# Values of two strided attention patterns by seven half-size products instead of eight, with sums of weights kept in DRAM

## Chip, core and metric

One core of a Trainium2 chip runs the whole program: a hybrid layer (block 1), then two layers of attention and retention (block 2), for 512 tokens of width 1024. The metric is device time in microseconds (us) of one execution; the lower, the better. TensorE is called PE, VectorE DVE, ScalarE ACT, GpSimd POOL, and SyncE SP: SP issues nearly all DMAs, in one queue and in its program order.

## What is computed

Only one projection of block 2 is touched. In each of its two layers the normalized input `h` (512 x 1024) is multiplied by `w_in`, and the columns called `va` (1536 of them) are the attention's values, 512 for each of three patterns:

```
ATT_PATTERNS = ((128, 1), (512, 4), (2048, 16))
...
h = rmsnorm(x, norm_w) * (1.0 + scale[:, None, :]) + shift[:, None, :]
proj = h @ w_in
qa, ka, va, za, qr, kr, vr, zr, ga, gr = jnp.split(proj, SPLIT_POINTS, axis=-1)
...
qa, ka, va = qa.reshape(att_shape), ka.reshape(att_shape), va.reshape(att_shape)
```

The first pattern is dense (g=0 in the kernel); the other two (g=1 and g=2) have strides of 4 and 16 and want their tokens regrouped by the token's number modulo 4. So the product in question is `h` (512 x 1024) times 1024 columns of weights, once in each layer.

## The kernel before

Every fp32 product is made of three products of rounded parts: `split` (lines 140 to 148) copies a tile to fp32r on ACT, the high part, and subtracts that copy from the tile on DVE, the low part; then high x high, high x low and low x high are summed in PSUM. A matmul with 512 columns is the unit of PE's work.

Weights come in tiles of 128 x 1024 fp32, 512 KB. `load_w` (line 187) takes one: a DMA into a raw tile `wr`, of which there are two, then `wh` on ACT (L144) and `wl` on DVE (L145), of which there are four pairs and, for each fifth load, one more. A raw tile is free for the next DMA when its `wl` is made. A pair is free when the last matmul that reads it has run. In nearly all stages one weight tile serves 24 matmuls.

`T_` (line 222) makes an output of 512 tokens by 512 columns in four PSUM banks, one for each 128 tokens, from four weight tiles. `attention_v` (line 961) calls it once for g=0, with all four weight tiles loaded first and each group of tokens started as its norm comes ready, and then, from inside `attention` (L1122), for g=1 and g=2 one weight tile after the other: 96 matmuls each, and for each group of 128 tokens a copy on ACT and four DMAs of 64 KB that regroup the tokens (L973, L975). Behind these come the q and k products of the heads (`w2_qk`).

In the first layer `rotary_tables` (line 925) makes sines and cosines for the retention, some 17 operations on DVE and two on ACT, just ahead of those products.

The feed-forward stage of block 1 (`ffn`, line 739) runs 44 weight tiles. Beside it a second task, `ada` (line 570), multiplies a vector by 25 MB of modulation weights on DVE: tiles `aw` of 256 KB through SP's queue, each followed by one DVE operation (L578). Tasks are generators that yield an estimated time; `tick` resumes them between matmuls. After that the framework orders the instructions of each engine by its own estimates, where `high_priority` pulls the weight loads ahead. What stands in an engine's queue behind an instruction that waits has to wait too.

Of the kernel before, what the change touches and what calls it, by code (L numbers as in the profile page):

```python
# [7 lines left out]
F32 = mybir.dt.float32  # L8
F32R = mybir.dt.float32r
I32 = mybir.dt.int32  # L10
AF = mybir.ActivationFunctionType
# [4 lines left out]
P = 128  # L16
S = 512
D = 1024
# [32 lines left out]
class Block:  # L51
# [211 lines left out]
    def T2_(self, lhs, srcs, nk, done, room, mid=None, cut=None):  # L263

        npair = nk // 2
        banks = [[None] * 4, [None] * 4]

        def step(half, t, w, c, kk, a=0, b=512):
            k = 2 * c + kk
            o = slice(kk * 512 + a, kk * 512 + b)
            if banks[half][t] is None:
                banks[half][t] = self.pst()
            ps = banks[half][t][:, a:b]
            hi, lo = lhs(k, t, 0), lhs(k, t, 1)
# [12 lines left out]
        if mid:  # L290
            mid()
        spare = iter(room())
        sets = [(half, c) for half in range(2) for c in range(first[half], npair)]
        ws = {x: self.load_w(srcs[x[0]][x[1]], next(spare, None)) for x in sets}
        for t in range(4):
            for half in range(2):
                parts = (0, 256, 512) if cut and t == 3 and half else (0, 512)
                for a, b in zip(parts, parts[1:]):
                    if a:
                        banks[half][t] = None  # L300
                    for c in range(first[half], npair):
                        for kk in range(2):
                            step(half, t, ws[half, c], c, kk, a, b)
                    if len(parts) > 2:
                        cut(banks[half][t], a, b)
                    else:
                        done(t, half, banks[half][t])

    def room(self, x):

# [428 lines left out]
    def ffn(self, hf, fp, es_w):  # L739
        tc, nc, A, v = self.tc, self.nc, self.A, self.nc.vector  # L740
        f, th = [], {}
        es = ExitStack()
        pool = []

        def done(i, ps):
# [77 lines left out]
    def block2(self, h, es_w):  # L823
# [6 lines left out]
        for l in range(2):  # L830
# [4 lines left out]
            yp, e_ya = op("yatt")  # L835
            ya = self.new_op(yp, "ya", n=4)
            vp, e_v = op("attv")
            V = self.attention_v(l, h, vp, range(1))
# [117 lines left out]
        nc.scalar.activation(self.cos, k, AF.Sin)  # L956


    def attention_v(self, l, h, vp, gs, V=None, ap=None):

        V = {} if V is None else V
        for g in gs:
            if g:
                for c in range(4):
                    V[g, c] = vp.tile([P, 512], F32, tag="V", name=self.nm("V"), bufs=12)

            def done(t, ps):
                if g == 0:
                    V[g, t] = vp.tile([P, 512], F32, tag="V", name=self.nm("V"), bufs=12)
                    self.nc.scalar.activation(V[g, t], ps, AF.Copy)  # L970
                    return
                x = ap.tile([P, 512], F32, tag="qk", name=self.nm("Vt"), bufs=4)
                self.nc.scalar.activation(x, ps, AF.Copy)  # L973
                for c in range(4):
                    self.nc.sync.dma_start(out=V[g, c][t * 32:t * 32 + 32, :], in_=x[c:P:4, :])  # L975

            self.T_(self.tok(h), self.A["w2_va"][l, g], 8, done, outer=0 if g else 4, ready=None if g else h.ready)
        return V

    def attention(self, l, h, ap, vp, V, ya, mrg):  # L980

# [133 lines left out]
        def finish(rows_):  # L1115
            while not all(r.done for r in rows_):
                yield 0.5
            yield from join()
            for hd in range(4):
                yield from out(hd)  # L1120

        self.attention_v(l, h, vp, (1, 2), V, ap)  # L1122
        for hd in range(4):
            head(hd, range(3))
        self.spawn(finish(list(self.tasks)))
        for i in range(12):
            if i % 3 == 0:
# [526 lines left out]
```

## Time and profile before

| | us |
|---|---|
| median of 3 runs | 2517.1 (2516.03 to 2517.49) |
| the profiled execution | 2515.06 |
| its span in the trace | 2513.3 |
| PE busy | 2493.3 (99%) |
| DVE busy | 1403.6 (56%) |
| ACT busy | 1062.7 (42%) |
| POOL busy | 99.2 (4%) |

The granted clock of PE is at its full level in all 40 slices of the page. The page puts 92% of the chain that ended last on PE. Of the moved bytes 283 MB go through SP's queue, at a mean of 114 GB/s, and most in the slices of the feed-forward stage (about 780 to 1043 us), at some 200 GB/s. The products of g=1 and g=2 lie at 1201 to 1245 us in the first layer and 1866.5 to 1911 us in the second.

### The profile page before, as it was taken

What the parts mean: (1) busy time and instruction counts of PE and PEld (TensorE: products, weight loads), DVE (VectorE), ACT (ScalarE), POOL (GpSimd) and SP (SyncE); (2) the same over time, 40 slices, a digit from 0 to 9 for tenths busy, and PEclk for the clock granted to TensorE, in tenths of its full rate; (3) what the DMA queues carried; (4) which work ended last, traced back from release to release, by engine and by line L of the source; (5) the groups of instructions that cost most, each with busy time, mean ns of one, the idle gap of its engine ahead of it and who ended that gap; (6) DMA issues with size and microseconds to landing.
All of it is one profiled execution on the core that took longest, in us unless ns stands there. A gap on an engine that the chain in (4) does not pass through costs nothing.

```text
span 2513.3 us, 31228 instructions
## 1 busy us (share of the span) xinstructions
PE 2493.3 (99%) x11850; PEld 2056.5 (82%) x11850; DVE 1403.6 (56%) x2651; ACT 1062.7 (42%) x1829; POOL 99.2 (4%) x104
## 2 busy tenths in 40 slices
PE   9999999999999999999999999999999999999998
PEld 7877777878888888888888888888888888888887
DVE  6567665776656777626333436664452343375635
ACT  4477666875334333324343432323233334233323
POOL 0023332000000000000000000000000000000000
PEclk9999999999999999999999999999999999999999
DMA  5522222323345666534422122222443222322233
GB/s 181 173 80 78 70 71 93 95 88 110 118 131 182 211 194 216 184 132 142 134 93 92 62 90 82 86 76 92 144 141 126 89 79 68 101 70 98 68 100 118
DMA packets 99129, 286.47 MB, mean 114 GB/s; under 512 B 13193, under 2 KB 19209, under 8 KB 98850
## 3 DMA queue, kind: packets, MB, share of 16 engines
q1 hardware_dynamic: 98256, 283.22, 35.2%
q8 instruction: 93, 1.52, 0.3%
q10 hardware_dynamic: 722, 1.25, 0.1%
q14 instruction: 58, 0.48, 0.1%
HBM read 259.16 MB, written 12.61 MB: 108 GB/s over the span
## 4 chain that ended last, share of the span: by engine, by line
PE 92%; DVE 3%; ACT 2%; DMA 2%; issue 1%; POOL 0%; ACTq 0%; POOLq 0%; DVEq 0%
PE ps L129 89%; PE ps L138 3%; DMA wr<-in_w_out_dram 1%; DVE wl L145 1%; ACT S L1416 1%; ACT wh L144 0%; DMA wr<-in_w_o_dram 0%; DVE yr L145 0%; POOL S L1423 0%; DVE PTl L145 0%; DVE S L1410 0%; ACT S L1421 0%; DMA x<-in_x_dram 0%; DVE xc L629 0%; DMA wr<-in_nsa_wv_dram 0%
## 5 line engine op out<-in xcount | busy, mean ns | idle before, releaser
L129 PE MATMUL ps<-h,wh 128*128 128x512 f32 (+1 forms) x4000 | 1242.8, 391 | 0.0
L129 PEld LDWEIGHTS ps<-h,wh 128*128 128x128 f32 x4000 | 733.5, 188 | 139.3 <-issue 5.1
L145 DVE TENSOR_TENSOR wl<-wr,wh 128x1024 fp32r<-128x1024 f32 x383 | 469.1, 1225 | 556.1 <-ACT wh L144 555.2
L144 ACT ACTIVATE wh<-wr 128x1024 fp32r<-128x1024 f32 x383 | 405.6, 1059 | 871.4 <-PE ps L129 658.3
L129 PE MATMUL ps<-h,wl 128*128 128x512 f32 (+1 forms) x2000 | 772.9, 386 | 0.0
L129 PEld LDWEIGHTS ps<-h,wl 128*128 128x128 f32 x2000 | 375.9, 188 | 75.7 <-DVE wl L145 0.4
L129 PE MATMUL ps<-wh,h 128*128 128x512 f32 x832 | 261.2, 392 | 0.3 <-ACT h L144 0.3
L129 PEld LDWEIGHTS ps<-wh,h 128*128 128x128 f32 x832 | 156.6, 188 | 33.6 <-DVE h L145 0.8
L129 PE MATMUL ps<-wl,h 128*128 128x512 f32 x416 | 162.4, 390 | 0.0
L129 PE MATMUL ps<-y,wh 128*128 128x512 f32 x384 | 119.3, 391 | 0.0
L129 PEld LDWEIGHTS ps<-wl,h 128*128 128x128 f32 x416 | 78.4, 188 | 16.1
L129 PE MATMUL ps<-wh,f 128*128 128x512 f32 x288 | 89.6, 389 | 0.0
L129 PEld LDWEIGHTS ps<-y,wh 128*128 128x128 f32 x384 | 71.5, 188 | 14.4
L129 PE MATMUL ps<-yr,wh 128*128 128x512 f32 x256 | 78.8, 389 | 0.0
L1416 ACT ACTIVATE S<-S,sm 128x128 f32<-128x128 f32 (+3 forms) x128 | 70.2, 550 | 19.0 <-DVE sm L1414 18.8
L1423 POOL TENSOR_SCALAR S<-S,sm 128x128 f32<-128x128 f32 (+3 forms) x64 | 69.6, 1099 | 214.0 <-ACT Q L144 78.2
L145 DVE TENSOR_TENSOR PTl<-ps,PTh 128x512 fp32r<-128x512 f32 (+1 forms) x96 | 65.0, 683 | 22.4 <-ACT PTh L144 21.6
L144 ACT ACTIVATE PTh<-ps 128x512 fp32r<-128x512 f32 (+1 forms) x96 | 56.1, 588 | 49.0 <-PE ps L138 44.0
L129 PE MATMUL ps<-y,wl 128*128 128x512 f32 x192 | 74.7, 389 | 0.0
L578 DVE SCALAR_TENSOR_TENSOR acc<-aw,cact,acc 128x512 f32<-128x512 f32 x96 | 71.8, 748 | 4.7 <-DMA acc<-in_b_ada_dram 2.7
L1014 DVE CUSTOM_DVE_ANT_0 P<-ps,c_masks 128x128 f32<-128x128 f32 (+1 forms) x96 | 31.2, 325 | 65.0 <-PE ps L129 62.9
L1410 DVE CUSTOM_DVE_ANT_0 S<-ps,c_mask 128x128 f32<-128x128 f32 (+3 forms) x128 | 59.9, 482 | 8.6 <-PE ps L129 7.5
(337 smaller groups left out, 3047.9 us busy)
## 6 DMA issues: line engine op xcount, KB each, us to landing
aw<-in_w_ada_dram SPq DMA_DIRECT2D x96, 256.0 KB, 3.9
wr<-in_w_qk_dram SPq DMA_DIRECT2D x48, 512.0 KB, 3.5
wr<-in_w_ffn_in_dram SPq DMA_DIRECT2D x44, 512.0 KB, 3.8
wr<-in_w_g_dram SPq DMA_DIRECT2D x32, 512.0 KB, 3.5
wr<-in_w_qr_dram SPq DMA_DIRECT2D x32, 512.0 KB, 3.6
wr<-in_w_mg_dram SPq DMA_DIRECT2D x24, 512.0 KB, 3.6
wr<-in_w_va_dram SPq DMA_DIRECT2D x24, 512.0 KB, 4.6
wr<-in_w_ffn_out_dram SPq DMA_DIRECT2D x22, 512.0 KB, 3.9
```

Source lines behind the costliest of these rows:

```text
L129: self.nc.tensor.matmul(out, a, b, start=start, stop=stop, skip_group_check=True)
L138: self.nc.tensor.transpose(out, in_, self.ident[:k, :k])
L144: nc.scalar.activation(hi, src, AF.Copy)
L145: nc.vector.tensor_sub(lo, src, hi.bitcast(F32))
L578: v.scalar_tensor_tensor(acc, w, self.cact[:, k:k + 1], acc, op0=ALU.mult, op1=ALU.add)
L1014: v.tensor_tensor_reduce(dst, pv, mask, 1.0, -3e38, ALU.add, ALU.max, mx[:, n:n + 1])
L1410: v.tensor_tensor_reduce(Pt[:, o], ps[:, o], self.mask[:, 512 - N:], 1.0, -3e38, ALU.add, ALU.max, mx[:, h:h + 1])
L1416: nc.scalar.activation(Ps[h], Ps[h], AF.Exp, scale=0.125, bias=nm_[:, h:h + 1], accum_out=ls[:, h:h + 1])
L1423: nc.gpsimd.tensor_scalar(Ps[h], Ps[h], r[:, h:h + 1], None, op0=ALU.mult)
```

## The change

With halves of the tokens, of the summed width and of the columns, a product of 2 x 2 blocks can be made of seven products of blocks instead of eight, if sums and differences of blocks are formed on either side. `TS_` does this (the form with 15 additions): three products read blocks of `h` or of the weights as they are and share results; of the weights four sums are needed and of `h` four sums.

- The four sums of the weights, for both layers, are made by a new task `weight_sums` beside `ada` in the feed-forward stage: eight chunks of four loads of 256 KB, four subtractions on POOL and four stores of 256 KB to a DRAM tile `vas`.
- The sums of `h` are made by `strided_v` in each layer: eight tiles R put the high and low parts together (four on DVE, four on POOL), four more operations on each engine add them, and eight splits (`Sx`) round them for PE.
- Each of the seven products has 24 matmuls (256 tokens, 512 of the summed width, 512 columns) and takes two weight tiles, from `w2_va` or from `vas`. Results are shared through tiles X: two copies on ACT, ten additions on DVE that read PSUM.
- `rotary_tables` moves behind the q and k products.

```diff
+        product("a", A(0, 0), B(0, 0), True, lambda t, ps: nc.scalar.activation(e[t], ps, AF.Copy))
+        product("a", A(1, 0), B(0, 1), False, lambda t, ps: done(t, 0, ps))
+        product("b", Sx(1), Tx(1), True, lambda t, ps: v.tensor_add(u2[t], e[t], ps))
+        product("b", Sx(2), Tx(2), False, lambda t, ps: v.tensor_add(u3[t], e[t], ps))
+        product("b", A(1, 1), Tx(3), False, last(e, 2, 0))
+        product("c", Sx(0), Tx(0), True, last(u3, 2, 1))
+        product("c", Sx(3), B(1, 1), False, last(u2, 0, 1))
...
+            ws = [self.load_w(y) for y in w]
+            for t in range(2):
...
+                for k in range(4):
...
+                    self.mm(ps, hi, wh[:, o], start and k == 0, False)
+                    self.mm(ps, hi, wl[:, o], False, False)
+                    self.mm(ps, lo, wh[:, o], False, k == 3)
...
+    def weight_sums(self, src, dst, pool):
...
+                for half, c in ((0, i), (1, i), (1, 2 + i), (0, 2 + i)):
+                    q.append(pool.tile([P, 512], F32, tag=f"q{len(q)}", name=self.nm("q"), bufs=1))
+                    self.nc.sync.dma_start(out=q[-1], in_=src[half][c][:, o])
+                yield 3.0
+                b11, b12, b22, b21 = q
+                g.tensor_sub(b11, b12, b11)
+                g.tensor_sub(b12, b22, b12)
+                g.tensor_sub(b22, b22, b11)
+                g.tensor_sub(b21, b21, b22)
+                yield 7.0
+                for j, t in enumerate((b11, b22, b12, b21)):
+                    self.nc.sync.dma_start(out=dst[2 * j + i][:, o], in_=t)
+                yield 2.5
...
                 self.ada_init()
                 self.spawn(self.ada(pool[0], 1.2))
+                self.spawn(weights())
...
-                if l == 0:
-                    self.rotary_tables(ap)
                 self.attention(l, h, ap, vp, V, ya, mrg)
...
-        self.attention_v(l, h, vp, (1, 2), V, ap)
+        self.strided_v(l, h, vp, V, ap)
         for hd in range(4):
             head(hd, range(3))
+        if l == 0:
+            self.rotary_tables(ap)
```

The order of instructions around the touched products in the first layer, first SP's queue before, from the third weight tile of g=1 to the first copies out (`wr` are weight loads, `V` the regrouping DMAs):

```order
L191 DMA wr_11048<-in_w_va_dram 128x1024
L191 DMA wr_11078<-in_w_va_dram 128x1024
L191 DMA wr_11108<-in_w_va_dram 128x1024
L191 DMA wr_11138<-in_w_va_dram 128x1024
L191 DMA wr_11192<-in_w_qk_dram 128x1024
L191 DMA wr_11225<-in_w_qk_dram 128x1024
L975 DMA V_10888<-Vt_11016 32x512
```

And now, from the second weight tile of product 3 to the first of product 5 (six `V` rows like the last one shown are left out):

```order
L191 DMA wr_11152<-vas_7670 128x1024
L191 DMA wr_11186<-vas_7670 128x1024
L1074 DMA V_10992<-X_11059 32x512
L191 DMA wr_11192<-vas_7670 128x1024
L1074 DMA V_10993<-X_11059 32x512
...
L191 DMA wr_11224<-vas_7670 128x1024
```

Eight weight loads that stood ahead of all regrouping DMAs are fourteen now, and seven of those DMAs stand between the second load of product 4 (wr_11192) and the first of product 5 (wr_11224).

DVE's queue at the end of the touched products before, where nothing but weight splits stands:

```order
L145 TENSOR_TENSOR wl_11111<-wr_11108,wh_11110 128x1024
L145 TENSOR_TENSOR wl_11141<-wr_11138,wh_11140 128x1024
L145 TENSOR_TENSOR wl_11195<-wr_11192,wh_11194 128x1024
L145 TENSOR_TENSOR wl_11228<-wr_11225,wh_11227 128x1024
L145 TENSOR_TENSOR wl_11261<-wr_11258,wh_11260 128x1024
```

And now, from product 6's second weight tile (wl_11279) to the first q product's (wl_11367); the rows with X add a result that PE has just finished, ps_11282 and ps_11300 being the two banks of products 6 and 7:

```order
L145 TENSOR_TENSOR wl_11279<-wr_11276,wh_11278 128x1024
L340 TENSOR_TENSOR X_11058<-X_11058,ps_11282 128x512
L340 TENSOR_TENSOR X_11058<-X_11058,ps_11300 128x512
L145 TENSOR_TENSOR wl_11321<-wr_11318,wh_11320 128x1024
L145 TENSOR_TENSOR wl_11327<-wr_11324,wh_11326 128x1024
L340 TENSOR_TENSOR X_11057<-X_11057,ps_11282 128x512
L340 TENSOR_TENSOR X_11057<-X_11057,ps_11300 128x512
L145 TENSOR_TENSOR wl_11367<-wr_11364,wh_11366 128x1024
```

The split of product 7's first weight tile (wl_11321) stands behind both additions that wait for the end of product 6, and that of the first q product (wl_11367) behind both that wait for the end of product 7.

In the feed-forward stage SP's queue reads now, from the fifth weight tile on (`q` are loads for the sums of weights, `aw` and `acc` belong to `ada`):

```order
L191 DMA wr_8135<-in_w_ffn_in_dram 128x1024
L640 DMA aw_8106<-in_w_ada_dram 128x512
L640 DMA aw_8115<-in_w_ada_dram 128x512
L369 DMA vas_7670<-q_8008 128x512
L191 DMA wr_8178<-in_w_ffn_in_dram 128x1024
L369 DMA vas_7670<-q_8012 128x512
L369 DMA vas_7670<-q_8010 128x512
L369 DMA vas_7670<-q_8014 128x512
L360 DMA q_8154<-in_w_va_dram 128x512
...
L191 DMA wr_8233<-in_w_ffn_in_dram 128x1024
```

The stores, which wait for POOL, and the next chunk's loads, which wait for the stores, stand among the weight loads; from the first `q` to the last `vas` there are eight such chunks and nineteen weight loads of `w_ffn_in`.

## Rows read from the trace of the kernel before

**Rows 1.** The page: span, and busy time of the engines.
```profile
span 2513.3 us, 31228 instructions
...
PE 2493.3 (99%) x11850; PEld 2056.5 (82%) x11850; DVE 1403.6 (56%) x2651; ACT 1062.7 (42%) x1829; POOL 99.2 (4%) x104
```

**Rows 2.** Timeline of PE: start us, length us, engine, line, operation, out<-in, count.
```profile
1143.29 5.60 PE L129 MATMUL ps<-f,f 128*128 128x512 f32 x24
1148.73 0.39 PE L129 MATMUL ps<-wh,f 128*128 128x512 f32 x1
```

**Rows 3.** Windows: length, busy us (instructions) by engine, clock, DMA share, GB/s.
```profile
1201.00:1245.00 44.00, 44.00 (x195) 36.42 (x195) 16.07 (x19) 16.66 (x20) 0.00 (x0) 1.00 0.47 153
1866.00:1911.00 45.00, 45.00 (x200) 37.25 (x200) 11.34 (x10) 14.94 (x19) 0.00 (x0) 1.00 0.46 155
```

**Rows 4.** Timeline of SP's DMA issues in the second layer.
```profile
1864.97 11.98 SPq L191 DMA_DIRECT2D wr<-in_w_va_dram x5
...
1887.05 10.03 SPq L975 DMA_DIRECT2D V<-Vt x16
```

**Rows 5.** Timeline of ACT, second layer; in brackets idle time and its releaser.
```profile
1862.63 1.06 ACT L144 ACTIVATE wh<-wr 128x1024 fp32r<-128x1024 f32 x1 [0.76 <-PE ps L129]
...
1866.71 0.60 ACT L970 ACTIVATE V<-ps 128x512 f32<-128x512 f32 x1 [1.66 <-PE ps L129]
1868.39 1.06 ACT L144 ACTIVATE wh<-wr 128x1024 fp32r<-128x1024 f32 x1 [1.08 <-DMA wr<-in_w_va_dram]
1870.38 1.06 ACT L144 ACTIVATE wh<-wr 128x1024 fp32r<-128x1024 f32 x1 [0.93 <-DMA wr<-in_w_va_dram]
1874.28 1.06 ACT L144 ACTIVATE wh<-wr 128x1024 fp32r<-128x1024 f32 x1 [2.85 <-DMA wr<-in_w_va_dram]
```

**Rows 6.** Timeline of DVE, second layer.
```profile
1856.69 1.29 DVE L145 TENSOR_TENSOR h<-ps,h 128x512 fp32r<-128x512 f32 x2 [3.54 <-ACT h L144]
...
1869.48 1.23 DVE L145 TENSOR_TENSOR wl<-wr,wh 128x1024 fp32r<-128x1024 f32 x1 [3.17 <-ACT wh L144]
...
1875.38 1.23 DVE L145 TENSOR_TENSOR wl<-wr,wh 128x1024 fp32r<-128x1024 f32 x1 [2.68 <-ACT wh L144]
```

**Rows 7.** Timeline of ACT, five loads issued back to back.
```profile
1130.84 1.06 ACT L144 ACTIVATE wh<-wr 128x1024 fp32r<-128x1024 f32 x1 [1.64 <-DMA wr<-in_w_ffn_out_dram]
1134.15 1.06 ACT L144 ACTIVATE wh<-wr 128x1024 fp32r<-128x1024 f32 x1 [2.25 <-DMA wr<-in_w_ffn_out_dram]
1136.97 1.06 ACT L144 ACTIVATE wh<-wr 128x1024 fp32r<-128x1024 f32 x1 [1.76 <-DMA wr<-in_w_va_dram]
```

**Rows 8.** Timelines of PE and DVE in the feed-forward stage: a product's end, what follows.
```profile
988.48 0.39 PE L129 MATMUL ps<-h,wl 128*128 128x512 f32 x1
...
988.90 0.69 DVE L759 TENSOR_TENSOR ft<-ft,ps 128x512 f32<-128x512 f32 x1 [0.80 <-PE ps L129]
...
990.96 0.69 DVE L148 SCALAR_TENSOR_TENSOR f<-ft,f 128x512 fp32r<-128x512 f32 x1
991.57 0.68 DVE L145 TENSOR_TENSOR acc<-acc,acc 128x512 fp32r<-128x512 f32 x1
```

**Rows 9.** Window around the join of the attention's heads, first layer.
```profile
1390.00:1420.00 30.00, 30.00 (x162) 24.15 (x161) 18.83 (x51) 12.34 (x25) 0.00 (x0) 1.00 0.22 71
```

**Rows 10.** Windows of the feed-forward stage: 106 us, and its fullest 5 us.
```profile
890.00:895.00 5.00, 5.00 (x24) 4.14 (x23) 3.76 (x5) 1.64 (x3) 0.00 (x0) 1.00 0.99 333
813.00:919.00 106.00, 106.00 (x571) 92.19 (x570) 78.81 (x108) 38.79 (x54) 0.00 (x0) 1.00 0.65 210
```

**Rows 11.** Timelines of POOL and DVE where both subtract or add in SBUF.
```profile
296.02 0.73 POOL L1474 TENSOR_TENSOR yraw<-Z,W 64x256 f32<-64x256 f32 x1 [2.16 <-DMA W<-Z]
296.82 1.60 POOL L1475 TENSOR_TENSOR yraw<-Z,W 64x256 f32<-64x256 f32 x1
...
296.06 1.77 DVE L145 TENSOR_TENSOR wl<-wr,wh 128x1024 fp32r<-128x1024 f32 x1
```

**Rows 12.** Timeline of ACT in the feed-forward stage: what a weight split waits for.
```profile
988.73 1.06 ACT L144 ACTIVATE wh<-wr 128x1024 fp32r<-128x1024 f32 x1 [3.89 <-PE ps L129]
```

More of the change, by code (lines that the diff above doesn't have):

```diff
@@ new lines, in weight_sums @@
+    def weight_sums(self, src, dst, pool):
+        g = self.nc.gpsimd
+        for i in range(2):
+            for o in (slice(0, 512), slice(512, D)):
+                q = []
+                for half, c in ((0, i), (1, i), (1, 2 + i), (0, 2 + i)):
[11 more added lines that the diff above has]
+                yield 2.5
@@ L743, in ffn, with weights @@
         pool = []
+        self.va_sums = [self.dp.tile([8, P, D], F32, tag=f"vas{l}", name=f"vas{l}") for l in range(2)]
+        def weights():
+            for l in range(2):
+                yield from self.weight_sums([A["w2_va"][l, g] for g in (1, 2)], self.va_sums[l], pool[0])
         def done(i, ps):
@@ L837, in block2 @@
             vp, e_v = op("attv")
-            V = self.attention_v(l, h, vp, range(1))
+            V = self.attention_v(l, h, vp)
             self.wait()
@@ L956, in rotary_tables, with attention_v, done @@
         nc.scalar.activation(self.cos, k, AF.Sin)
[L959 to L977, printed above, removed]
-        return V
+    def attention_v(self, l, h, vp):
+        V = {}
+        def done(t, ps):
+            V[0, t] = vp.tile([P, 512], F32, tag="V", name=self.nm("V"), bufs=12)
+            self.nc.scalar.activation(V[0, t], ps, AF.Copy)
+        self.T_(self.tok(h), self.A["w2_va"][l, 0], 8, done, outer=4, ready=h.ready)
+        return V
@@ new lines, in strided_v, with done, sums @@
+    def strided_v(self, l, h, vp, V, ap):
+        nc, v, g_ = self.nc, self.nc.vector, self.nc.gpsimd
+        for g in (1, 2):
+            for c in range(4):
+                V[g, c] = vp.tile([P, 512], F32, tag="V", name=self.nm("V"), bufs=12)
+        R, H = {}, {}
+        for p in range(2):
+            for i, (kh, th) in enumerate(((1, 1), (0, 1), (0, 0), (1, 0))):
+                tag, n = ("qk", 4) if p == 0 else ("PT", 2) if i < 2 else ("s", 2)
+                r = R[p, kh, th] = ap.tile([P, S], F32, tag=tag, name=self.nm("R"), bufs=n)
+                part = (slice(None), slice(4 * kh + 2 * p, 4 * kh + 2 * p + 2), slice(256 * th, 256 * th + 256))
+                (v if th else g_).tensor_add(r.rearrange("p (k q) -> p k q", k=2), h.hi[part].bitcast(F32), h.lo[part].bitcast(F32))
+        for p in range(2):
+            a11, a12, a21, a22 = (R[p, kh, th] for th in range(2) for kh in range(2))
+            v.tensor_add(a22, a21, a22)
+            g_.tensor_sub(a21, a11, a21)
+            v.tensor_sub(a11, a22, a11)
+            g_.tensor_sub(a12, a12, a11)
+            R[p] = a22, a11, a21, a12
+        for j in (1, 2, 0, 3):
+            for p in range(2):
+                hi, lo = (ap.tile([P, 4, P], F32R, tag="P1", name=self.nm("Sx"), bufs=8).rearrange("p a b -> p (a b)")
+                          for _ in range(2))
+                self.split(hi, lo, R[p][j])
+                H[j, p] = hi, lo
+        X = [ap.tile([P, 4, 256], F32, tag="P0", name=self.nm("X"), bufs=4).rearrange("p a b -> p (a b)") for _ in range(4)]
+        place = lambda j, t: X[j][:, t * 512:t * 512 + 512]
+        def done(t, half, z):
+            if t < 2 and half == 0:
+                x = place(3, t)
+                nc.scalar.activation(x, z, AF.Copy)
+            else:
+                x = z
+            for c in range(4):
+                nc.sync.dma_start(out=V[1 + half, c][t * 32:t * 32 + 32, :], in_=x[c:P:4, :])
+        def sums(j, k, t, lo):
+            o = (k % 2) * 256 + t * P
+            return H[j, k // 2][lo][:, o:o + P]
+        self.TS_(h, [self.A["w2_va"][l, g] for g in (1, 2)], self.va_sums[l], sums, place, done)
```

22 lines of the change are left out of this document (added).

## The prediction

> **What bounds the kernel now.** I read the page first: PE is busy 2493.3 of 2513.3 us [rows 1], so time is won only by taking matmuls away or lost by making PE wait. Next PE's timeline for the price of a matmul: 24 of them with 512 columns take 1148.73 - 1143.29 = 5.44 us, 0.2267 us each [rows 2]. Then the windows of the two stages that change: PE is busy all through both, 44.00 of 44 and 45.00 of 45 us [rows 3], so there is no waiting there to get rid of, and any wait that comes is a loss in full. Last SP, ACT and DVE in these stages, for how fast weight tiles can be made ready [rows 4 to 7], and the feed-forward stage, for what room it has [rows 10 to 12].
>
> **What goes.** In each layer 8 x 24 = 192 matmuls become 7 x 24 = 168. 2 x 24 x 0.2267 = 10.9 us of PE's time go. That is the whole gain. Eight copies to Vt on ACT become two copies out and two of results to keep, off PE's path.
>
> **What comes: weight tiles at twice the rate.** Before, a tile served 24 matmuls (5.44 us); now a product has two tiles for 24 matmuls, one per 2.72 us. What can two raw tiles supply? In the second layer five loads stand back to back in SP's queue [rows 4]. The first is issued at 1864.97, when a raw tile comes free, its `wh` begins at 1868.39 [rows 5], its `wl` ends at 1869.48 + 1.23 = 1870.71 [rows 6]: 5.7 us. The raw tile then free carries the load whose `wh` begins at 1874.28 and whose `wl` ends at 1876.61: 5.9 us. Two raw tiles give two loads in each 5.9 us; the product that eats them takes 5.44. At 1130.84 and 1136.97, two loads apart, it is 6.1 us [rows 7]. So the supply is 0.5 us a product too slow once the lead is used up, and PE has to wait for it.
>
> Load by load for the second layer, from the start of product 1, at 1866.5 (the last product of g=0 is copied at 1866.71 [rows 5]). `h` is complete at 1856.69 + 1.29 = 1858.0 [rows 6]. DVE now does eight sums of 128x512 first, 0.61 us apart as at 990.96 and 991.57 [rows 8], 4.9 us; POOL's four sums beside them may add 2. After one split of `Sx` the second load's `wl` is done at about 0.7 instead of before 0 (its `wh` begins at 1862.63 [rows 5]), the third's at 2.5. From there each raw tile needs 5.9 us: loads 4, 6 and 8 are ready at 6.6, 12.5 and 18.4, loads 5 and 7 at 8.4 and 14.3. The second load of product p is wanted after half of its first 12 matmuls, at 5.44 x (p - 1) + 1.36 + 0.2: 7.0, 12.4 and 17.9. PE waits 0.1 and then 0.5, in sum 0.6 us by product 4. Load 9 is issued behind seven regrouping DMAs; SP needs 10.03 / 16 = 0.63 us for each [rows 4], 4.4 us from load 8's issue at 12.5, so it goes at 16.9 and is ready at 22.8, wanted at 21.8 + 0.6 + 0.2. Load 10, behind it and a split on DVE, is ready at 24.6, wanted at 23.9: 0.7 more. Load 12 costs 0.4. Through product 6 this is 1.7 us a layer.
>
> **What comes: two places where DVE's queue is in the way.** Product 7's first `wl` stands behind the additions that need the end of product 6, and the first q product's `wl` behind those that need the end of product 7. At 988.48 + 0.39 a product's last matmul ends and DVE reads its bank from 988.90, 0.2 us after the next matmul could have started [rows 8]. With an addition of 0.6 and a `wl` of 1.2 (1.23 long [rows 6]) the weights are there 2.0 us after the product's end; meanwhile PE can run the two matmuls that need `wh` alone, 0.45 us. It waits 1.6 us at each place, 3.2 a layer. This wait holds even if the loads are early, since the order is fixed.
>
> Together 4.9 a layer, 9.8 us. Bounds: only the two queue waits, 6.4 us in all; above, 6.5 us in place of 5.9 for a raw tile (ACT and DVE have the splits of `Sx` and the copies between, and the 64 KB transfers share the DMA engines), 0.6 us more in each of five products: 16 us. The trace has no stage that takes tiles at this rate for long, so this stays an estimate; I take 9.8, nearest to the measured 5.7 to 6.1.
>
> **What comes: the rotary tables later.** They needed 10 us of DVE where it was idle; now their 17 operations fall among those of the join of the heads, where DVE is busy 18.83 of 30 us [rows 9]. 28.8 of 30 just fits. PE's transposes wait for this chain. I take 1 us, between 0 (PE has the gate products to run) and 2.
>
> **What comes in the feed-forward stage.** 32 subtractions of 128x512 on POOL, 64 DMAs of 256 KB (16.8 MB), in the course of nineteen weight tiles, about 106 us. Cover: a weight split waits for PE to free a pair of four [rows 12], so its tile is wanted three products later, 3 x 5.44 - 2.3 = 14 us; SP's loads may lag about that. I cost it at 1 us, between 0 and 12; the 12 is worked out below.
>
> Sum: -10.9 + 9.8 + 1 + 1 = +0.9 us, from 2515.06 of the profiled execution to 2516; against the median of 2517.1, which lies 2 us above it, 2518. Nearly all of the gain turns into waits on weights.
>
> **Rivals.**
>
> *The supply keeps up.* Then the waits of the loads are absent and those of DVE's queue shrink to one a layer, say: -10.9 + 3.2 + 1 = -6.7, 2510; with no wait at all 2506. For it: at 1134.15 and 1136.97 two loads follow each other in 2.8 us [rows 7], nearly the 2.72 wanted. Against it: that is one gap of two, and the pair takes 6.1.
>
> *The feed-forward stage is overrun (slower).* One mechanism: POOL's subtractions and DVE's two-input operations get in each other's way, and SP's queue, which waits for POOL before each store, holds the weight loads behind it. When POOL and DVE both read two SBUF tiles, DVE's `wl` took 1.77 us instead of 1.23, and POOL's second addition 1.60 instead of 0.73 [rows 6, 11]: the sum of both works, almost as if one after the other. A POOL operation of twice the columns takes up to 1.46 us, 32 of them 47 us. DVE is busy 78.81 of 106 us there [rows 10], which leaves 27: if DVE is held up for all of POOL's time it ends 20 us late. The DMA engines moved 210 GB/s x 106 = 22 MB there; with 16.8 more, at the 333 GB/s of the fullest 5 us [rows 10], it takes 117 us: 11 us late. From 14 us of lateness on PE waits. Both in full would cost 31 - 14 = 17, DVE's alone 6, the middle 12: 2518 - 1 + 12 = 2529. Against it: DVE need not be held for all of POOL's time, and `ada` can fall behind without PE waiting.
>
> The Trainium skill (SBUF - State Buffer, Who interferes with whom) states that a VectorE instruction with two SBUF inputs contends with a GpSimd instruction that reads SBUF, and that the loser blocks fully. The collision in rows 11 agrees as far as one case can. By that rule alone the 47 us fall on DVE or on POOL in full, which is the case just worked out; by the mean of rows 11, 0.55 us for each of 32, DVE would lose 18 us and stay within its 27.
>
> *The stages cost more than they save.* With 16 us of waits instead of 9.8: 2524. For it: the lead may be gone sooner, if POOL's sums of `h` come late. Then waits begin at product 1.
>
> **How the numbers follow.** What a measurement of this kernel tells from no change is about 0.2%, 5 us. The forecast, within 5 us of before, 0.47; the supply keeps up 0.18, faster; feed-forward overrun 0.24, slower; stages dearer 0.11, slower. So faster 0.18, same 0.47, slower 0.35. The likeliest case's own range is 2513 to 2522. Reaching into the others, 2509 to 2530: below lies the supply without any wait, above the overrun in full.
>
> **What would show it.** 48 matmuls of 128x512 fewer. In both stages PE idle time before L129 released by `wl` L145 of some 5 us a layer, from product 2 on, with the longest just behind the additions L340. If PE is busy in full there, the supply step is wrong. `wh` starts two loads apart at 5.9 us or more. In the feed-forward stage POOL operations of 1.4 us alone and up to 3 beside DVE, `wl` of up to 2 us, and PE without waits; waits on `wl` there mean the overrun. An idle PE at the transposes of the heads in the first layer alone would be the rotary tables. The forecast is wrong if the time leaves 2512 to 2522.

## The result, and the profile after

The changed kernel is slower: 2537.95 us, median of 5 runs (2535.33 to 2539.62), against 2516.03 (2513.23 to 2517.49) for before on the same chip; ratio 1.0089, 95% interval 1.0074 to 1.0103. The forecast was 2518, range 2509 to 2530. The page of its profiled execution, with the rows that answer to [rows 1] (busy us of each engine), and further down the share of the chain that ended last:

```profile
span 2537.8 us, 31371 instructions
...
PE 2495.3 (98%) x11802; PEld 2047.6 (81%) x11802; DVE 1473.5 (58%) x2715; ACT 1084.0 (43%) x1852; POOL 177.4 (7%) x152
...
PE 78%; DVE 7%; DMA 6%; ACT 4%; issue 3%; POOL 1%; SPq 0%; ACTq 0%; DVEq 0%; POOLq 0%
```

There are 48 matmuls fewer, as announced, and yet the span is 24.5 us longer. PE's part of the last chain was 92% before; DVE and DMA have come in.

Where the time goes can be read off closely, since PE runs the same matmuls in the same order but for the 24 fewer per layer. The table counts matmuls in PE's timeline and compares the time between the same two of them with before; a negative number is time won. "Layer 1" and "layer 2" are the strided stage with the heads' products behind it (and for layer 1 the stretch from the feed-forward stage on); of each, -5.4 are the matmuls that went. "Rest" is all else, and scatters by some us from trace to trace.

| traced execution, us against before | feed-forward | layer 1 | join, layer 1 | layer 2 | rest | sum |
|---|---|---|---|---|---|---|
| changed kernel | +7.1 | +9.5 | +2.1 | +6.3 | -0.7 | +24.3 |
| e2_rotary_alone | 0.0 | +0.1 | +2.2 | 0.0 | -0.1 | +2.2 |
| e1_no_sums | 0.0 | +7.6 | +2.1 | +6.1 | +2.6 | +18.4 |
| f3_sums_pool_only | +0.7 | +7.2 | +2.1 | +6.4 | +2.9 | +19.3 |
| f5_small_dma | 0.0 | +7.4 | +2.2 | +6.0 | +0.8 | +16.4 |
| f2_sums_dma_only | +0.5 | +7.1 | +2.2 | +5.9 | +0.9 | +16.6 |
| f6_dma_only_again | +1.4 | +7.0 | +2.2 | +6.6 | -0.7 | +16.5 |
| e6_sums_poolq | +0.4 | +7.2 | +2.1 | +5.4 | +0.9 | +16.0 |
| f4_slow_pace | 0.0 | +6.6 | +2.2 | +5.0 | -0.1 | +13.7 |
| e3_loads_ahead | +6.8 | +10.4 | +2.2 | +6.2 | +1.3 | +26.8 |
| e4_regroup_pool | +7.6 | +10.3 | +2.1 | +8.5 | -0.6 | +28.0 |
| e5_four_raw | +4.5 | +2.3 | +2.2 | +2.8 | -0.8 | +11.0 |
| e7_raw_dve | +3.3 | -0.6 | +2.2 | -1.7 | +1.8 | +5.0 |
| e8_raw_first_head | +9.1 | -4.0 | +2.2 | -4.2 | +1.6 | +4.8 |
| c5_all | 0.0 | -3.9 | 0.0 | -4.1 | +3.0 | -5.0 |
| c6_all_ahead | +9.7 | -3.2 | 0.0 | -4.1 | -1.6 | +0.8 |
| c8_all_slow | +0.2 | -3.9 | 0.0 | -4.1 | +0.4 | -7.3 |
| c9_all_sp_slow | 0.0 | -3.9 | 0.0 | -4.0 | +0.3 | -7.7 |
| c10_adds_first | 0.0 | +2.0 | 0.0 | -3.3 | +0.6 | -0.7 |

**The strided stages.** The window of the second layer's stage, which answers to [rows 3] (length, busy us by engine, clock, DMA share, GB/s):

```profile
1881.00:1933.00 52.00, 45.82 (x190) 34.39 (x188) 30.77 (x33) 21.31 (x27) 5.12 (x4) 1.00 0.52 159
```

PE was busy in full before; here 6.2 of 52 us are idle, and a matmul that has waited also costs more than its 0.227 us (0.34 from the start of the one at 1253.11 us, after 0.76 of wait, to the next). The groups of PE in this window say who is late (busy us, mean ns, then idle time before them and its releasers):

```profile
L129 PE MATMUL ps<-wh,Sx 128*128 128x512 f32 x64 | 20.6, 396 | 1.0 <-ACT wh L144 0.6 <-DVE X L340 0.5
L129 PE MATMUL ps<-wh,h 128*128 128x512 f32 x61 | 19.5, 394 | 1.0 <-ACT X L344 0.9
L129 PE MATMUL ps<-wl,Sx 128*128 128x512 f32 x32 | 12.8, 404 | 1.7 <-DVE wl L145 1.7
L129 PE MATMUL ps<-wl,h 128*128 128x512 f32 x31 | 12.4, 401 | 2.4 <-DVE wl L145 2.4
```

Why `wl` is late from the start stands in DVE's and POOL's timelines (start, length):

```profile
1876.65 2.50 DVE L1049 TENSOR_TENSOR R<-h,h 128x512 f32<-128x512 f32 x4
1879.06 1.29 DVE L1052 TENSOR_TENSOR R<-R,R 128x512 f32<-128x512 f32 x2
1881.54 2.36 DVE L1054 TENSOR_TENSOR R<-R,R 128x512 f32<-128x512 f32 x2 [1.19 <-POOL R L1053]
1883.99 1.60 DVE L145 TENSOR_TENSOR Sx<-R,Sx 128x512 fp32r<-128x512 f32 x1
1885.52 2.32 DVE L145 TENSOR_TENSOR wl<-wr,wh 128x1024 fp32r<-128x1024 f32 x1
...
1892.39 1.23 DVE L145 TENSOR_TENSOR wl<-wr,wh 128x1024 fp32r<-128x1024 f32 x1 [1.61 <-ACT wh L144]
...
1898.21 1.22 DVE L145 TENSOR_TENSOR wl<-wr,wh 128x1024 fp32r<-128x1024 f32 x1 [1.95 <-ACT wh L144]
...
1904.77 1.23 DVE L145 TENSOR_TENSOR wl<-wr,wh 128x1024 fp32r<-128x1024 f32 x1 [2.33 <-ACT wh L144]
```
```profile
1879.88 2.86 POOL L1053 TENSOR_TENSOR R<-R,R 128x512 f32<-128x512 f32 x2 [10.52 <-issue]
1883.37 3.38 POOL L1055 TENSOR_TENSOR R<-R,R 128x512 f32<-128x512 f32 x2 [0.63 <-DVE R L1054]
```

DVE's L1054 writes over a tile that POOL's L1053 still reads, so it stands still for 1.19 us; then the two engines work side by side, and DVE's subtraction takes 1.2 instead of 0.6 us, `Sx` 1.60 instead of 0.68, `wl` 2.32 instead of 1.23. The second load is ready at 1887.84, 2.65 us after product 1's start at 1885.19, where the forecast had it at 0.7. The last three rows are the splits of the fourth, sixth and eighth load. From there the raw tiles pass the delay on, as ACT's timeline shows:

```profile
1891.30 1.06 ACT L144 ACTIVATE wh<-wr 128x1024 fp32r<-128x1024 f32 x1 [3.41 <-DMA wr<-in_w_va_dram]
1892.26 0.58 ACT L344 ACTIVATE X<-ps 128x512 f32<-128x512 f32 x1
```

The fourth load could be issued only when the second's split had freed its raw tile, and ACT stood 3.41 us at its `wh`, with the copy `X` behind it that product 2's first matmul needs.

**The feed-forward stage.** The window that answers to the 106 us of [rows 10], and the stretch in which the waits begin, in SP's timeline:

```profile
813.00:919.00 106.00, 106.00 (x571) 92.20 (x570) 77.14 (x96) 35.93 (x50) 36.97 (x24) 1.00 0.86 284
```
```profile
923.52 0.39 SPq L191 DMA_DIRECT2D wr<-in_w_ffn_in_dram  x1
928.71 5.07 SPq L369 DMA_DIRECT2D vas<-q  x4
...
934.62 0.40 SPq L191 DMA_DIRECT2D wr<-in_w_ffn_in_dram  x1
```

The DMA engines go from 0.65 to 0.86 busy, 284 for 210 GB/s. SP stands from 923.9 to 928.7 in front of the stores of sums, and two weight loads are issued 11.1 us apart, where a tile is eaten in 5.44. That is one of three things on PE's path here; the others are late transfers and POOL's work beside DVE's. Both stand in front of PE's longest wait in this stage, 2.16 us (timelines of DVE, POOL and PE):

```profile
944.17 4.62 DVE L641 SCALAR_TENSOR_TENSOR acc<-aw,cact,acc 128x512 f32<-128x512 f32 x3 [1.29 <-DMA aw<-in_w_ada_dram]
948.71 1.21 DVE L145 TENSOR_TENSOR wl<-wr,wh 128x1024 fp32r<-128x1024 f32 x1
...
944.94 1.62 POOL L365 TENSOR_TENSOR q<-q,q 128x512 f32<-128x512 f32 x1
946.64 1.61 POOL L366 TENSOR_TENSOR q<-q,q 128x512 f32<-128x512 f32 x1
...
949.98 0.50 PE L129 MATMUL ps<-h,wl 128*128 128x512 f32 x1 [2.16 <-DVE wl L145]
```

The transfers `aw` land late, and the three operations of `ada` that they release run beside POOL's subtractions: 4.62 us, where one alone takes 0.75. The split `wl` that PE waits for stands behind them. After this wait 8 matmuls run at the lower clock, 1.6 of the 7.1 us.

### The profile page after: what moved, and what is told of

Its sections match the earlier page's. It is cut to its first block, busy times and chain, and to the rows that moved or that the text cites. A ratio compares the mean times of both kernels' runs of the same rounds, so it can differ in the third digit from the quotient of the medians.

```text
span 2537.8 us, 31371 instructions
## 1 busy us (share of the span) xinstructions
PE 2495.3 (98%) x11802; PEld 2047.6 (81%) x11802; DVE 1473.5 (58%) x2715; ACT 1084.0 (43%) x1852; POOL 177.4 (7%) x152
## 4 chain that ended last, share of the span: by engine, by line
PE 78%; DVE 7%; DMA 6%; ACT 4%; issue 3%; POOL 1%; SPq 0%; ACTq 0%; DVEq 0%; POOLq 0%
PE ps L129 76%; PE ps L138 3%; DVE wl L145 2%; ACT wh L144 1%; DMA wr<-in_w_ffn_in_dram 1%; DMA wr<-vas 1%; DMA aw<-in_w_ada_dram 1%; DMA wr<-in_w_va_dram 1%; ACT S L1520 1%; DMA wr<-in_w_out_dram 1%; DVE acc L641 1%; DMA wr<-in_w_o_dram 0%; DVE xn L396 0%; DMA amul<-adar 0%; DMA wr<-in_w_qk_dram 0%
## 5 line engine op out<-in xcount | busy, mean ns | idle before, releaser
L145 DVE TENSOR_TENSOR wl<-wr,wh 128x1024 fp32r<-128x1024 f32 x395 | 492.9, 1248 | 509.5 <-ACT wh L144 508.6
L144 ACT ACTIVATE wh<-wr 128x1024 fp32r<-128x1024 f32 x395 | 417.8, 1059 | 825.8 <-PE ps L129 563.4
L129 PE MATMUL ps<-wh,h 128*128 128x512 f32 x672 | 213.1, 393 | 3.0 <-ACT X L344 2.5
L129 PEld LDWEIGHTS ps<-wh,h 128*128 128x128 f32 x672 | 126.5, 189 | 31.7 <-ACT X L344 3.4
L129 PE MATMUL ps<-wl,h 128*128 128x512 f32 x336 | 132.0, 393 | 3.9 <-DVE wl L145 3.8
L641 DVE SCALAR_TENSOR_TENSOR acc<-aw,cact,acc 128x512 f32<-128x512 f32 x96 | 79.2, 824 | 9.9 <-DMA aw<-in_w_ada_dram 8.4
L129 PEld LDWEIGHTS ps<-wl,h 128*128 128x128 f32 x336 | 63.3, 189 | 18.8 <-DVE wl L145 6.1
L1049 POOL TENSOR_TENSOR R<-h,h 128x512 f32<-128x512 f32 x8 | 15.9, 2020 | 884.2 <-PE ps L129 648.9
```

Of the source, the lines that this page charges most:

```text
L129: self.nc.tensor.matmul(out, a, b, start=start, stop=stop, skip_group_check=True)
L144: nc.scalar.activation(hi, src, AF.Copy)
L145: nc.vector.tensor_sub(lo, src, hi.bitcast(F32))
L641: v.scalar_tensor_tensor(acc, w, self.cact[:, k:k + 1], acc, op0=ALU.mult, op1=ALU.add)
L1049: (v if th else g_).tensor_add(r.rearrange("p (k q) -> p k q", k=2), h.hi[part].bitcast(F32), h.lo[part].bitcast(F32))
```

## The experiments

All edits are to the changed kernel, if not said otherwise; times are compared by the table above.

### The rotary tables

**e2_rotary_alone**: the kernel before, with the call of `rotary_tables` put behind the heads' products.

> The kernel before, with one part of the change: the rotary tables emitted behind the products of the heads. Theory: their operations stand in ACT's and DVE's queues among those of the join of the heads, and PE's transposes there wait: the stretch from the fourth head's products to the last gate product of the first layer is 2.1 us longer than before (66.6 us), all else the same. Rival, that stretch is longer because the strided stage in front of it ends later: 0 here.

Measured: +2.16 us in the join and nothing elsewhere, the same +2.1 to +2.2 as in every kernel with this order. But it is hardly DVE that is late: PE waits 0.16 us for its `mc`, and 1.38 us for ACT's `t`. ACT's timeline in this kernel:

```profile
1402.33 1.28 ACT L949 ACT_TABLE_LOAD   x1
1403.62 0.63 ACT L949 ACTIVATE sin<-ra 128x512 f32<-128x512 f32 x1
1404.27 1.28 ACT L1137 ACT_TABLE_LOAD   x1
1405.57 0.60 ACT L1137 ACTIVATE m<-ps 128x512 f32<-128x512 f32 x1
1406.18 1.28 ACT L954 ACT_TABLE_LOAD   x1
1407.47 0.63 ACT L954 ACTIVATE cos<-rk 128x512 f32<-128x512 f32 x1
1408.01 0.57 ACT L1063 ACTIVATE t<-ps 4x512 f32<-4x512 f32 x1
```

Two sines among tanh and exp change ACT's function table three times, 1.28 us each, and the copy `t` that PE's transposes wait for stands behind them.

### The feed-forward stage

**e1_no_sums**: no `self.spawn(weights())`; the strided products read tiles of `w2_va`.

> Changed kernel without the sums of weights in the feed-forward stage (no DMAs, no POOL subtractions; the products that want sums read w2_va itself, so the values are other ones). Theory: these sums cost the feed-forward stage 7 us and 0.7 us after it, and nothing else: PE's feed-forward stretch is back at 159 us (it was 166), the two strided stages stay as they are, total 2538 - 7.7 = 2530. Rival A, the stage is late for another reason: 2538. Rival B, the sums' tiles in DRAM are also slower to load in the strided stages: those get shorter too, total below 2526.

Measured: 2532.65 us median against 2514.93, ratio 1.0069 (1.0052 to 1.0086). The stage is back at 0.0 and the strided stages keep their waits. So 7 us belong to the sums of weights, and the rest does not.

**f2_sums_dma_only** (without the four `g.tensor_sub`) and **f3_sums_pool_only** (the subtractions, on tiles set to zero, without DMAs; with no transfer to wait for they run in one sweep from 819 to 876 us, where the changed kernel has them from 823 to 948):

> The 64 DMAs of the sums without the 32 POOL subtractions (what is stored is the weights themselves). Theory D, the transfers load the DMA engines (their share rose from 0.62 to 0.9): the feed-forward stretch stays 5 us or more longer than before. Theory Q, SP's queue stands still because the stores wait for POOL and the weight loads wait behind them: with no POOL to wait for the stretch is at most 3 us longer. Theory C, POOL and DVE get in each other's way: 0 to 1 us longer.

> The 32 POOL subtractions at the same places, on four tiles that are set to zero once, without the DMAs; the products read w2_va itself. Theory C (POOL and DVE collide): 5 us or more longer than before in the feed-forward stretch. Theories D and Q: 0 to 1 us longer; DVE's operations that read two SBUF tiles are still stretched (weighted sum of ada 0.91 instead of 0.75 us), but DVE has room for it.

Measured: +0.5 and +0.7. POOL's work by itself costs PE one wait at 878 us, though DVE's splits beside it take up to 2.3 us, so theory C falls as a cause by itself. DMAs by themselves cost little.

**e6_sums_poolq**: `self.nc.sync.dma_start` becomes `g.dma_start` for loads and stores of the sums.

> All as in the changed kernel, but the 64 DMAs of the sums go through POOL's own queue instead of SP's. Theory Q: the weight loads of SP no longer stand behind a store that waits for POOL, the feed-forward stretch loses at most 2 us of its 7; total about 2532. Theory D: the bytes are the same, it stays 5 us or more longer, total 2536 to 2540. Theory C: the same as D.

Measured: +0.4, one time of 2530.5. That looked like theory Q, until two later kernels with this edit and the same order in that stage lost 0.0 (c5_all) and 9.7 us (c6_all_ahead). One trace was not enough here.

**f5_small_dma**:

```
-dma_start(out=q[-1], in_=src[half][c][:, o])
+dma_start(out=q[-1][:, :64], in_=src[half][c][:, o.start:o.start + 64])   # stores likewise
```

> The changed kernel with the 64 DMAs of the sums in the same places and with the same waits, but each moving 64 of its 512 columns; POOL's 32 subtractions stay whole (the products read w2_va itself, so the values are other ones). Theory D, the bytes: the feed-forward stretch is within 0.5 us of before. Theory Q, the waits in SP's queue hold the weight loads behind them: 3 us or more longer than before, as in the five traces so far that have them (3.3 to 7.6).

**f6_dma_only_again** and **f4_slow_pace** (`yield 3.0, 7.0, 2.5` become `4.5, 9.5, 4.0`):

> The same as f2_sums_dma_only once more, since c5_all and c6_all_ahead with the same order of work up to that stage lost 0.0 and 9.7 us in it. If 0.5 us was typical of the DMAs without POOL, it is under 1 us again (theory Q: the waits for POOL are needed for a loss). If it was luck, 3 us or more (theory D).

> The changed kernel with the sums of weights at a slower pace: 18 instead of 12.5 us a step of the planner's clock, the same operations over some 145 us instead of 100. Theory D: the DMA engines' share falls from about 0.89 to about 0.8 and the feed-forward stretch loses 1 us or less. Theory Q: the waits are the same, 3 us or more.

Measured: 0.0, +1.4 and 0.0. The windows 843 to 950 us of the changed kernel, of f5_small_dma, of f6_dma_only_again and of f4_slow_pace, in this order:

```profile
843.00:950.00 107.00, 102.94 (x451) 83.79 (x449) 81.54 (x93) 33.45 (x45) 43.68 (x28) 1.00 0.90 309
```
```profile
843.00:950.00 107.00, 107.00 (x474) 88.63 (x473) 97.03 (x104) 36.93 (x49) 44.41 (x27) 1.00 0.71 227
```
```profile
843.00:950.00 107.00, 106.19 (x468) 87.38 (x468) 72.18 (x97) 33.94 (x46) 0.00 (x0) 1.00 0.90 315
```
```profile
843.00:950.00 107.00, 107.00 (x473) 88.63 (x473) 85.58 (x100) 33.30 (x47) 29.96 (x20) 1.00 0.84 286
```

With the same order and waits and an eighth of the bytes (DMA share 0.71) there is no wait, though POOL works as long as in the changed kernel and DVE is busy 97 of 107 us. At a share of 0.90 the bytes alone cost 0.5 and 1.4 us; bytes, POOL's subtractions and the waits for them in SP's queue together cost 3.3 to 9.1 (six traces, shares of 0.87 to 0.90). At 0.84 with all of them there is no loss. So nothing is lost without the bytes in time: theory D. What makes them dearer are two things that come together with POOL's work and that f2 and f6 take away together: the waits in SP's queue (theory Q) and the collisions with DVE (theory C). The collisions are on PE's path: in all six traces PE waits 1.9 to 2.2 us for the same split as at 949.98 above, behind the same three operations beside POOL; in f6 and f2, without POOL, this wait is 0.81 and 0.09 us. With the sums' DMAs in POOL's queue, so without Q, four traces (e6, c5, c6, c8) lose 0.4, 0.0, 9.7 and 0.2. How much belongs to Q and how much to C is not shown.

### The strided stages

**e3_loads_ahead**, the order alone:

```
-ws = [self.load_w(y) for y in w]
+ws = got.pop(0)
+got.append([self.load_w(y) for y in nxt])    # nxt: the next product's tiles
```

> The changed kernel with each product's two weight loads emitted at the start of the product before it, and those of product 1 before the sums of h. Theory O, order of the queues: most of the waits come since a weight split stands behind an addition or a copy that needs the product's end, or behind the sums of h. The two strided stages with the heads' products behind them cost 12 us over before in the last four runs (about 23 us of waits against 10.9 won); here at most 6 over before, the waits at the first matmul of products 2 and 7 and of the first q product are gone. Theory S, supply: two raw tiles can't carry it whatever the order: at least 10 over before.

**e4_regroup_pool**: the regrouping `dma_start` of `strided_v` on `g_` instead of `nc.sync`.

> The changed kernel with the 64 regrouping DMAs of the strided values issued by POOL instead of SP. Theory: in SP's queue they stand ahead of weight loads and cost the waits at products 5 and 7 (0.9 + 0.7 + 1.0 us a layer): the strided stages come 4 to 6 us shorter in both layers together. Theory O (the order on DVE and ACT alone) and theory S: at most 1 us shorter.

**e5_four_raw**: in the strided stage (`self.rx`) raw tiles alternate between the two of `wp` and the memory of the fifth pair.

```
+if self.rx and self.nr % 4 > 1:
+    raw = self.wx.tile([P, 1024], F32R, tag=("wh", "wl")[self.nr % 2], bufs=1).bitcast(F32)
```

> The changed kernel with four raw tiles in the strided stage instead of two (the fifth weight pair's memory; the pairs stay four). Theory S: a raw tile is no longer what the loads wait for, the strided stages and the heads' products lose at least 6 us of the 12 that they lie over before. Theory O: the splits stand in DVE's and ACT's queues where they stood, at most 3 us shorter. Rival: without the fifth pair the loads wait for a pair instead, and the stage is longer than in the changed kernel.

Measured, both layers together, against +15.8 in the changed kernel and +11.6 to +13.7 in seven others with the same strided order: e3 +16.6, e4 +18.8, e5 +5.1. In e3 PE runs 7.3 us at the lower of its two clock levels behind its waits, in e4 11.5 us, which cost them 3.4 and 5.4 us; without that they are at 13.2 and 13.4. Theory O falls: an order with the loads ahead gives nothing while two raw tiles feed them. Nor does the regrouping on POOL, against the 4 to 6 us expected: the two stages by themselves are 0.9 and 0.7 us shorter and the wait of some 1.5 us at the first q product is gone in both layers, but the heads lose 4.4 and 5.2 us, for 2.7 and 2.2 in the changed kernel. Two more raw tiles alone take some 10 us off: theory S holds.

**e7_raw_dve**: e5 and

```
-g_.tensor_sub(a21, a11, a21)
+v.tensor_sub(a21, a11, a21)
```

> The kernel with four raw tiles, and besides it one of POOL's two subtractions of sums of h (R of the second and first quarter) done by DVE, so that DVE's next subtraction doesn't wait for POOL to have read its operand. Theory P: with the raw tiles there, what is left at product 1 (2.9 us in layer 0, 2.5 us and a stretch at half clock of 1.7 in layer 1) comes from DVE standing still for POOL in front of the weight split: these waits shrink to 1 us or less a layer, the two stages together are 5 us shorter than with four raw tiles alone. Rival: DVE gets 0.6 us more work twice and is late anyway: no gain, or up to 1 us worse.

Measured: the two stages with their heads -2.3 us instead of +5.1, the waits at product 1 gone. The 5 us expected were 7.4 (1.6 of them a stretch at the lower clock in e5). DVE's timeline: its subtractions of sums (L1058 is the one taken from POOL) now run without a gap and at 0.6 us each, and the first `wl` follows at once.

```profile
1866.74 1.28 DVE L1058 TENSOR_TENSOR R<-R,R 128x512 f32<-128x512 f32 x2
1867.94 1.29 DVE L1059 TENSOR_TENSOR R<-R,R 128x512 f32<-128x512 f32 x2
1869.15 1.22 DVE L145 TENSOR_TENSOR wl<-wr,wh 128x1024 fp32r<-128x1024 f32 x1
```

**e8_raw_first_head**: e7, and `self.rx`, which switches the four raw tiles on, stays true through the first head's products.

> The kernel of e7_raw_dve with the four raw tiles kept through the first head's six products. There PE still waits 1.8 us a layer at the third product of the first head: its load is issued behind 17 to 20 regrouping DMAs of SP's queue (0.63 us each), and its wh stands behind a copy on ACT that ends with the second product. Theory: with raw tiles free earlier that load goes out ahead of the regrouping and the wait is gone: the heads' stretch is 1.5 to 3 us a layer shorter than in e7_raw_dve (there +3.3 and +2.4 over before). Rival: SP's order keeps the regrouping first: no change.

Measured: the heads' stretches are 3.4 and 2.5 us shorter, the sums of the two layers -4.0 and -4.2. What was in the way shows in e7's SP and ACT timelines, 17 regrouping DMAs ahead of the third load, and its `wh` behind the copy of the second product:

```profile
1904.96 10.95 SPq L1079 DMA_DIRECT2D V<-X  x17
1916.01 1.00 SPq L195 DMA_DIRECT2D wr<-in_w_qk_dram  x2
```
```profile
1922.20 0.60 ACT L1136 ACTIVATE qk<-ps 128x512 f32<-128x512 f32 x1 [4.84 <-PE ps L129]
1922.70 2.00 ACT L144 ACTIVATE wh<-wr 128x1024 fp32r<-128x1024 f32 x2
```

### All together

**c5_all** is e8 with e6's queue, and with the rotary operations spawned as a task ahead of the heads, their scratch in the tiles "PT" and "s" that come free in the strided stage. **c6_all_ahead** adds e3's order.

```
-if l == 0:                      # behind the heads' products
-    self.rotary_tables(ap)
+if l == 0:                      # ahead of them; the function now yields between its operations
+    self.spawn(self.rotary_tables(tiles), 12.0)
```

> All causes found so far undone together, the seven products kept: the sums' DMAs on POOL's queue, four raw tiles in the strided stage and through the first head, the subtraction on DVE, and the rotary tables' operations spread from the strided stage's fifth product on (their scratch in tiles that come free there). Theory: feed-forward +0.4, the stretch behind it 0, the strided stages and the heads' products -3 (of -10.9, four waits of 2 us a layer or less left), the join 0: about 2.5 us less than before, ratio 0.999. Rival: the rotary operations in DVE's queue cost the splits of the strided stage 2 us and more, or the q loads lose what the stage wins: not under before.

> The same as c5_all, with each product's loads emitted one product ahead besides. Theory S (supply was the limit): the order adds nothing, within 1 us of c5_all in the strided stages. Theory O: once the supply is there the order is what is left, another 2 us or more shorter.

Measured: c5 2507.79 us against 2514.57, ratio 0.9976 (0.9967 to 0.9986), so 0.24% faster than before; the join is back at 0.0. Single runs reach 2515.68. c6 is no better in the strided stages (-3.2 and -4.1): with the supply there, order adds nothing. But it loses 9.7 us in the feed-forward stage, where PE stands at the two matmuls that `ada` puts into its queue:

```profile
935.75 0.80 PE L129 MATMUL ps<-acc,onesr 128*128 128x512 f32 x1 [3.58 <-ACT acc L144]
939.53 0.79 PE L129 MATMUL ps<-acc,onesr 128*128 128x512 f32 x1 [2.98 <-DVE acc L145]
```

The first of the two waits goes back to a transfer `aw` that DVE waits 3.80 us for; in front of the second DVE needs 1.69, 1.75 and 1.75 us for a `wl` and two splits beside POOL's subtractions, 1.22, 0.68 and 0.68 alone. Behind the waits PE runs 10 matmuls at the lower clock, 2.0 us.

**c8_all_slow** (c5 at f4's pace) and **c9_all_sp_slow** (the same with the sums' DMAs on SP):

> c5_all with the slower pace. Theory D: the feed-forward stage never overruns, all executions lie within 2 us of 2506 where those of c5_all reached from 2506.3 to 2515.7; ratio to before about 0.997. Rival: POOL's queue is late by itself now and then, single executions still lie 5 to 9 us higher.

> c5_all with the sums' DMAs back in SP's queue, at the slow pace of f4_slow_pace. In c8_all_slow the pace had no grip, POOL's queue had still done its DMAs by 940 us. Theory D (bytes in time): spread out over the whole stage the transfers cost nothing, every execution lies within 2 us of 2507, ratio 0.997. Rival Q: executions 3 us and more higher, since SP's queue waits for POOL again.

Measured: c8 2508.52 us, up to 2516.46; its DMA share at 903 to 933 us is still 0.94: in POOL's queue the slower pace does not hold the work back (the last subtraction starts at 939 us, in c5 at 940, in c9 at 981), and the rival, single runs that lie higher, came true. c9 2507.33 us (2506.01 to 2508.86) against 2514.43, ratio 0.9969 (0.9957 to 0.9980): in SP's queue the pace takes hold, and no run strays by more than 3 us. It beats both kernels. Its strided window:

```profile
1880.00:1920.00 40.00, 39.04 (x172) 31.81 (x172) 22.07 (x32) 14.15 (x16) 0.00 (x0) 1.00 0.53 185
```

**c10_adds_first**: c9, with `then(t, ps)` under `high_priority(offset=60)`.

> c9_all_sp_slow with the additions and copies at a product's end ahead of the weight splits in DVE's and ACT's queues. What was left in c5_all is a wait of 1.13 us a layer at product 4, whose first matmul of the second row half needs a bank that DVE's addition still has to read, behind a weight split. Theory: this wait goes, the two strided stages are 2 us shorter in all. Rival: the split that now stands behind the addition is late for product 5 instead: no gain.

Measured: 2513.32, ratio 0.9994 (0.9985 to 1.0003), not to be told from before. The strided stages are 1.3 and 1.4 us shorter, as expected, and the heads lose 7.2 and 2.1: results that come earlier let the planner put 24 regrouping DMAs in a row on SP, ahead of six q loads. SP's and PE's timelines:

```profile
1227.19 17.05 SPq L1085 DMA_DIRECT2D V<-X  x24
1244.34 8.45 SPq L195 DMA_DIRECT2D wr<-in_w_qk_dram  x6
```
```profile
1249.97 1.22 PE L129 MATMUL ps<-h,wh 128*128 128x512 f32 x2 [4.49 <-ACT wh L144]
```

## Why the prediction was wrong

- **What goes: right.** 48 matmuls, 10.9 us; with the waits removed the layers show -4.0 and -4.2 of -5.4 each, and in c10_adds_first the strided stages by themselves -5.3 each.
- **The waits on weights: right in kind, far too small.** The forecast was 9.8 us for both stages, 16 at most. With the heads' products behind them they cost 25.9 (15.8 - 0.8 in front of the stage + 10.9), 1.4 of it at the lower clock. Two terms failed. *The start*: the load-by-load account had the second load at 0.7; it came at 2.65, and the later loads stayed about 2 us behind the forecast ones (the fourth at 8.4 for 6.6, the sixth at 14.2 for 12.5, the eighth at 20.8 for 18.4). The sums of `h` were not at fault: redone, the 0.7 comes out with the 2 us for POOL in it (`h` complete at -8.5, then 4.9 + 2 for the sums, 0.6 on ACT and 0.6 on DVE for `Sx`, 1.2 for `wl`: 0.8), and DVE's eight sums, with the stand of 1.19 us, took 7.25 us for these 6.9. What was missed is what POOL does to the operations behind the sums: `Sx` and `wl`, costed at their length alone, ran beside POOL's last two subtractions and took 2.0 us longer. The rate of 5.9 us for two loads held at first, 5.8, and was then 6.6, over the 6.5 of the upper bound. *The places*: two for DVE's queue were counted. There were more, in ACT's queue (`X` behind a `wh` that waits for its transfer, 1.0 and 1.8 us at product 2) and in SP's (q loads behind the regrouping, which e8_raw_first_head shows at 3.4 and 2.5 us against e7_raw_dve).
- **Their price in the rivals: right side, wrong size.** "Lead gone sooner, if POOL's sums come late" was named, at 16 us in all and a chance of 0.11. The lead was gone sooner, though not since the sums came late, and the price was 25.9.
- **The feed-forward stage: the rival came true instead of the 1 us.** +7.1 for 1, bound 12. Its mechanism is what the traces show: bytes (share 0.90 at 309 GB/s), POOL against DVE, and SP's queue behind both. Its sum was not sound: it added two latenesses, with 6 us for the collisions alone, and each half alone costs little (f3_sums_pool_only 0.7, f5_small_dma 0.0, f2 and f6 0.5 and 1.4). They cost together, where late transfers leave DVE no room just when POOL runs beside it. POOL's and DVE's timelines in the changed kernel show two collisions:

```profile
844.43 1.29 POOL L363 TENSOR_TENSOR q<-q,q 128x512 f32<-128x512 f32 x1 [15.45 <-DMA q<-in_w_va_dram]
...
860.37 2.37 POOL L363 TENSOR_TENSOR q<-q,q 128x512 f32<-128x512 f32 x1 [9.34 <-DMA q<-in_w_va_dram]
```
```profile
844.63 1.64 DVE L145 TENSOR_TENSOR acc<-acc,acc 128x512 fp32r<-128x512 f32 x1 [0.70 <-ACT acc L144]
...
860.35 1.22 DVE L145 TENSOR_TENSOR wl<-wr,wh 128x1024 fp32r<-128x1024 f32 x1
```

  At 844 DVE lost (1.64 us, where [rows 8] have 0.68) and POOL kept its 1.29, at 860 POOL lost. The Trainium skill (SBUF - State Buffer, Who interferes with whom) states that the pair of ports which VectorE and GpSimd share is an exclusive lock, so that one of the two waits. These two cases agree: DVE lost 0.96 us while POOL still ran for 1.09, and POOL lost 1.08 while DVE ran its 1.22. Here DVE had room for its share of it, at 944 to 949 us it had not. "ada can fall behind without PE waiting" was wrong: its two products stand in PE's queue in order, and in c6_all_ahead PE waits 3.58 and 2.98 us at just them.
- **The rotary tables: size near (2.1 for 1, bound 2), reason wrong.** DVE's busy share was counted; most of it was ACT's table changes (1.38 of e2's 2.16 us in one wait).

The sum as it came: -10.9 + 25.9 + 0.8 + 7.1 + 2.1 - 0.7 = 24.3 us. The waits on weights by themselves break the range: with 25.9 and 0.8 in place of 9.8, and 1 us for each of the other two terms, the sum is 17.8 over before, 2535 for an upper end of 2530. Both rivals on the slow side came true together, and only one at a time was priced (2529 and 2524, jointly 2535). That this lies near the measured 2538 is in part luck: 16 stood for 25.9 and 12 for 7.1.

Open: why two executions of the same order at a DMA share of 0.89 and 0.87 lose 0.0 and 9.7 us in the feed-forward stage. Not tried alone: the subtraction on DVE with two raw tiles, and the sums of weights with their bytes but without collisions while SP still waits for them.

## What to carry to other kernels

Trading one matmul product for twice as many weight tiles is a question of buffers first: with two raw tiles the 2 us of lead that went at the start of this stage were not won back by the eighth load. Follow a new operation through every in-order queue that it enters, by reads and writes of its tiles, by what it pushes behind itself and by what it slows on the engine beside it; a collision that is free on average costs in full where the other engine has just been made late. And price rivals jointly where they don't exclude each other. A stage whose DMA engines are 0.9 busy should be measured in several executions, and its background transfers paced in a queue that holds them back.

## What the runs showed of the hardware

- After a wait PE's granted clock sometimes falls to its lower level (1.2 of 2.4 GHz), and matmuls take 0.43 instead of 0.227 us for 1.7 to 4.7 us. In c10_adds_first it follows the wait of 4.49 us; the window there, with the clock at 0.58:

```profile
1249.00:1256.00 7.00, 5.99 (x16) 4.29 (x17) 4.90 (x4) 4.09 (x4) 0.00 (x0) 0.58 0.83 278
```

  In e7_raw_dve PE waits 1.63 us twice and 0.96 us twice, and the clock stays; in the changed kernel it falls after the 2.16 us at 949.98. So in these traces a wait costs up to 2.2 us (0.47 of such a stretch, from 0.8) more than itself.
- A regrouping DMA of 64 KB takes 0.63 to 0.71 us of SP's queue (10.95 for 17, 17.05 for 24), 0.53 of POOL's (2.14 for 4).
